# A hybrid attention layer on one core: where the inverses' transposes, the key norm's second half and the value copies stand in the queues

## The chip, the cores and the metric

The kernel runs on one core of a Trainium2 chip. A core has a matrix engine (TensorE, PE in the profile), VectorE (DVE), ScalarE (ACT), GpSimd (POOL) and SyncE (SP), each with a queue of its own that is worked off in order, and 16 DMA engines that move data. The metric is the device time of one execution in microseconds; less is better.

## The reference, cut to what matters

One layer of a diffusion backbone: 1,024 latent tokens and 256 context tokens of width 1,024. One input projection feeds two groups of heads; the rest (output projection, feed-forward) follows.

```python
px = modulate(rms_norm(x, norm1_w), sh1, sc1) @ w_in      # latent tokens; pc: the same for the context
qkv = short_conv(p[..., :3 * DN_WIDTH], conv_w)           # group A: gated DeltaNet, 4 heads, chunks
kb = k * beta[..., None]
m = jnp.where(strict, jnp.einsum("bhncd,bhnmd->bhncm", kb, k) * decay, 0.0)
a_mat = jnp.eye(CHUNK) + m
u = triangular_solve(a_mat, v * beta[..., None], ...)     # and w, from kb: a scan over the chunks follows
q = rms_norm(q, q_norm_w) * NA_HEAD_DIM ** -0.5           # group B: neighbourhood attention, 8 heads
k = rms_norm(k, k_norm_w)
k_r = lax.dynamic_slice_in_dim(kg, r0, win_rows, axis=1)[:, :, key_cols]
v_r = lax.dynamic_slice_in_dim(vg, r0, win_rows, axis=1)[:, :, key_cols]
```

`key_cols` are four overlapping blocks of 32 of the 64 grid columns; the values of each block are gathered over all 16 rows.

## The kernel before, in words

**The stage.** The change lies in the input projection, from about 100 to 550 us. The activations stand in SBUF as fp32r pairs, `hh` + `hl` (a high part and what is left), and each product is made of three: `whi*hh`, `whi*hl`, `wlo*hh`. The projection is a list of jobs. A `Block` gives 128 columns, transposed: `k`, `q`, `v`, `z` of group A, `nk` and `nq` (keys and queries) of group B. A `Wide` gives half of group B's values, which go to the DRAM tile `nv_d`. A block over latent tokens alone has two segments of 512 columns, so 8 x 3 x 2 = 48 products in two PSUM banks (`blk`, four in all); `nk` has a third segment of 256. The order of jobs around the change is `nk` 0, 1, 2, the second `Wide`, `nk` 3, `nq` 0, 1, 2, `q` 0.

**What goes with a job.** The weights of the next job are loaded by SP (`wraw`, one buffer), cast by ACT (`whi`, L219) and split by POOL (`wlo`, L221). A finished block is copied out of PSUM by ACT (`evac`, L491) into `cacc` (two buffers) and squared (L532). Its `norm` follows a job later: PE sums the squares (`m<-cr`, `pr<-cr`), ACT takes Ln and Exp (L549 to L553), DVE multiplies (L556), ACT casts to fp16 (L561, L568), DVE subtracts for the low half (L562, L569), and SP stores both to `nk_d` or `nq_d`.

**Beside the jobs.** Generators are advanced by `bg.step` after each of a job's eight steps. `block_inverses` inverts the triangular 32x32 blocks of group A for all chunks, heads and both directions at once: `N` holds them with the 80 blocks on partitions; 30 pairs of DVE operations (L947, L949) and a memset of the diagonal (L952) do the elimination; PE transposes `N` back, 32 transposes into `m` banks (L106 in the profile, a helper's line), DVE copies them to `WK` (L961); then for each direction DVE transposes 32x32 blocks (L967), SP stores to `x_d` (L969), DVE scales by beta (L970) and SP stores that (L972). `preps` then prepares each chunk of the scan: `fetch` loads `e`, `kk` and the inverses `xc`; POOL masks `e`; ACT copies `xc` into `fx` (L1011) and takes the exponentials of `e` (L1015); DVE multiplies `kk` by `e` (L1016); PE multiplies (`pr<-fx,kk` in the profile), and three rounds follow (`pr<-y,kk`, each copied by DVE, L1036). `windows` copies the four column blocks of the values from `nv_d` to `vw_d`, in 16 DMAs on SP, from the second `Wide` on.

**What sets the order.** The program is written in the order of these generators; a scheduler then sets each engine's queue from its own estimate of times and from priorities. `keep_in_program_order` pins an instruction where it is written, `high_priority` lets one go ahead of what is written before it, `issue_after` puts one behind another in its queue.

**PSUM and memory.** The banks `m` and `pr` are two each. Buffers are reused under waits: a tile's next user waits for the last one's reads and stores. DMAs share eight semaphores in turn, and one waits for the DMA before it on its semaphore.

## Time and profile before

| | |
|---|---|
| median of 3 runs | 1506.96 us (1506.89 to 1511.58) |
| the profiled execution's own time | 1507.78 us |
| its span, first to last instruction | 1506.0 us |
| PE busy | 1449.8 us, 96% of the span |
| DVE, ACT, POOL busy | 1004.4, 696.2, 193.4 us |
| mean granted clock of PE | 0.994 |
| DMA | 267.35 MB, mean 178 GB/s |

The profile is of one execution; its rows give start, duration, engine, line, operation, tiles written and read, shapes and count, and in brackets how long the engine was idle before and what ended that. A row can merge equal instructions that follow each other. Line numbers in the profile are those of the kernel before; in the changed one the same statements stand 5 to 11 lines further down at first, and some 20 at the end of the stage.

### The profile page before, as it was taken

Reading aid. Unit: us, or ns where it says so; the run is one execution under the profiler, and the core shown is the slowest. Engines: PE = TensorE matmul, PEld = TensorE weight load, DVE = VectorE, ACT = ScalarE, POOL = GpSimd, SP = SyncE. Lnnn points to the kernel's source line nnn. Section 1 sums busy time; section 2 is a strip of 40 time slices with the busy share of each in tenths; the row PEclk is TensorE's granted clock in tenths of the full one; section 3 lists DMA queues with packets and bytes.
Section 4 is the critical chain, followed back from the end, with each engine's and each line's share of the span. In section 5 each row is a group of like instructions: output and inputs, shape, how many; then the busy total and the mean of one; then the engine's idle time right before and its main releaser. Section 6 shows DMA issues by size and latency. Waiting matters only on the chain.

```text
span 1506.0 us, 23093 instructions
## 1 busy us (share of the span) xinstructions
PE 1449.8 (96%) x8365; PEld 1201.0 (80%) x8365; DVE 1004.4 (67%) x1892; ACT 696.2 (46%) x1321; POOL 193.4 (13%) x223
## 2 busy tenths in 40 slices
PE   5999998899999999999989999999999999999998
PEld 2789787678877778887877878888888888888887
DVE  4886579455598427679966499666655557698642
ACT  6443461584266526566742374333333334354440
POOL 0154500343124221211100000000000000000000
PEclk9999999999999999999999999999999999999999
DMA  9377133555377799986349106333333334898742
GB/s 368 117 234 239 57 92 121 191 168 190 118 243 238 220 284 265 262 228 193 110 134 332 72 30 203 113 105 105 102 102 105 106 105 161 287 349 286 240 145 84
DMA packets 198851, 267.35 MB, mean 178 GB/s; under 512 B 15232, under 2 KB 106960, under 8 KB 197712
## 3 DMA queue, kind: packets, MB, share of 16 engines
q1 hardware_dynamic: 198016, 265.49, 54.7%
q8 instruction: 66, 1.08, 0.3%
q14 instruction: 49, 0.40, 0.1%
q10 hardware_dynamic: 720, 0.37, 0.1%
HBM read 201.01 MB, written 68.98 MB: 179 GB/s over the span
## 4 chain that ended last, share of the span: by engine, by line
PE 51%; DVE 6%; ACT 3%; DMA 2%; issue 1%; SPq 0%; ACTq 0%; DVEq 0%
PE ps L102 45%; PE sc L102 5%; PE sc L106 2%; DMA wad<-wa 1%; ACT pt L377 1%; ACT ex L365 1%; DVE ex L363 1%; DVE acc L255 1%; DVE x L1618 1%; DVE x L1594 0%; DVE ex L367 0%; DVE ulo L1449 0%; DVE lT L1589 0%; DVE ws L1444 0%; ACT x L1598 0%
## 5 line engine op out<-in xcount | busy, mean ns | idle before, releaser
L102 PE MATMUL ps<-hT,uhi 128*128 128x512 f32 x496 | 146.8, 390 | 0.8 <-DVE e L1739 0.7
L102 PE MATMUL ps<-lT,uhi 128*128 128x512 f32 x496 | 146.4, 389 | 0.0
L102 PE MATMUL ps<-hT,ulo 128*128 128x512 f32 x496 | 146.3, 389 | 0.0
L102 PE MATMUL blk<-hh,whi 128*128 128x512 f32 (+1 forms) x456 | 138.0, 393 | 2.4 <-ACT hh L748 1.7
L102 PE MATMUL blk<-hh,wlo 128*128 128x512 f32 (+1 forms) x456 | 129.7, 377 | 0.0
L102 PE MATMUL ps<-hB,uhi 128*128 128x512 f32 x436 | 129.1, 390 | 0.0
L102 PE MATMUL blk<-hl,whi 128*128 128x512 f32 (+1 forms) x456 | 129.0, 376 | 0.0
L102 PE MATMUL ps<-lB,uhi 128*128 128x512 f32 x436 | 128.8, 389 | 0.0
L102 PE MATMUL ps<-hB,ulo 128*128 128x512 f32 x436 | 128.8, 389 | 0.0
L1448 ACT CAST uhi<-ws 128x512 fp32r<-128x512 f32 x91 | 54.7, 622 | 145.5 <-PE ps L102 78.2
L1448 ACT CAST uhi<-wq 128x512 fp32r<-128x512 f32 x101 | 60.4, 621 | 132.8 <-PE ps L102 69.4
L1449 DVE TENSOR_TENSOR ulo<-wq,uhi 128x512 fp32r<-128x512 f32 x101 | 67.1, 687 | 65.6 <-ACT uhi L1448 36.4
L102 PEld LDWEIGHTS ps<-hT,uhi 128*128 128x128 f32 x496 | 93.0, 188 | 20.7 <-ACT uhi L1448 1.1
L102 PEld LDWEIGHTS ps<-lT,uhi 128*128 128x128 f32 x496 | 93.0, 188 | 19.7 <-DVE lT L1602 0.5
L102 PEld LDWEIGHTS ps<-hT,ulo 128*128 128x128 f32 x496 | 93.1, 188 | 19.4
L102 PEld LDWEIGHTS ps<-hB,uhi 128*128 128x128 f32 x436 | 81.8, 188 | 17.5 <-issue 0.5
L102 PEld LDWEIGHTS ps<-lB,uhi 128*128 128x128 f32 x436 | 81.8, 188 | 17.3 <-DVE lB L1602 0.4
L102 PEld LDWEIGHTS ps<-hB,ulo 128*128 128x128 f32 x436 | 81.8, 188 | 17.0
L102 PEld LDWEIGHTS blk<-hh,wlo 128*128 128x128 f32 x456 | 80.1, 189 | 17.6 <-issue 1.7
L102 PEld LDWEIGHTS blk<-hl,whi 128*128 128x128 f32 x456 | 80.7, 189 | 15.5
L102 PEld LDWEIGHTS blk<-hh,whi 128*128 128x128 f32 x456 | 76.5, 189 | 19.8 <-ACT hh L748 3.7
L1449 DVE TENSOR_TENSOR ulo<-ws,uhi 128x512 fp32r<-128x512 f32 x91 | 60.6, 685 | 36.2 <-ACT uhi L1448 28.0
(341 smaller groups left out, 3026.0 us busy)
## 6 DMA issues: line engine op xcount, KB each, us to landing
wq<-w_fo SPq DMA_DIRECT2D x99, 256.0 KB
wq<-w_gu SPq DMA_DIRECT2D x88, 256.0 KB
wad<-wa SPq DMA_DIRECT2D x64, 256.0 KB
t_d<-g SPq DMA_DIRECT2D x22, 512.0 KB
fr<-t_d SPq DMA_DIRECT2D x44, 256.0 KB
bt<-rpb SPq DMA_DIRECT2D x48, 192.0 KB
f_d<-g SPq DMA_DIRECT2D x33, 256.0 KB
fr<-f_d SPq DMA_DIRECT2D x33, 256.0 KB
```

Of the source, the lines that this page charges most:

```text
L102: i = nc.tensor.matmul(*args, **kw)
L106: i = nc.tensor.transpose(*args, **kw)
L255: dve.scalar_tensor_tensor(acc2, x, sc, acc2, op0=OP.mult, op1=OP.add)
L363: dve.tensor_tensor_reduce(ex, sc, bt, 1.0, -3.0e38, OP.add, OP.max, m[:, 0:1])
L365: act.activation(ex, ex, AF.Exp, bias=m[:, 1:2], accum_out=m[:, 2:3])
L377: act.copy(pt, sc)
L1448: act.copy(hi, self.raw[key])
L1449: dve.tensor_tensor(lo, self.raw[key], hi.bitcast(F32), OP.subtract)
L1618: dve.tensor_tensor(B[at][:, k], B[x][:, k], B.get(y, B["B11"])[:, k], OP.subtract)
```

## The change

1. The inverses' transposes wait for eight steps of the background instead of one, are pinned where they are written, eight after each of four steps of the job `nq` 1; DVE's copies get a high priority.
2. The block transposes and scalings of both directions follow the copies with a high priority. The result `ut` now lies in the memory of `N`.
3. `norm` is split: its second half (`split`: L556 to L574 of before) of the last key block (`nk` 3, `tail`) is written after the inverse is done and the first fetch is issued, and issued behind the last scaling; the query blocks' second halves up to `turn` go behind it too.
4. The first two fetches of `preps` come ahead of its loop, with three steps of pause.
5. The value copies: `vw_d` is laid out as four blocks of 512 keys x 512 columns, each is copied by one DMA of 16 runs of 64 KB on ACT's queue, one at every second step of `nk` 3.

```diff
-    vw_d = dram.tile([128, 4, 4, 512], F32, name="vw_d", tag="vw_d")
+    vw_d = dram.tile([4, 512, 512], F32, name="vw_d", tag="vw_d")
...
+                return self.split
+            def split(self):
+                acc, t0, i, r = self.acc, self.t0, self.i, self.r
+                isk = self.kind == "nk"
                 u = acc
                 dve.scalar_tensor_tensor(u[:, t0:], u[:, t0:], qkw[:, isk:isk + 1], r[:, t0:],
...
-                for _ in range(1):
+                for _ in range(8):
                     yield
...
-                        pe.transpose(p[:, i * P:(i + 1) * P], N[:P, :, :, i0 + i].rearrange("p b r -> p (b r)"),
-                                     ident[:P, :P])
-                    dve.tensor_copy(U[:, :, i0:i0 + 4], p[:, :4 * P].rearrange("p (i u) -> p u i", i=4))
+                        tc.keep_in_program_order(nc.tensor.transpose(
+                            p[:, i * P:(i + 1) * P], N[:P, :, :, i0 + i].rearrange("p b r -> p (b r)"),
+                            ident[:P, :P]))
+                    with tc.high_priority(offset=400):
+                        dve.tensor_copy(U[:, :, i0:i0 + 4], p[:, :4 * P].rearrange("p (i u) -> p u i", i=4))
...
-                    ut = g4.tile([128, NU, 32], F32, name="ut", tag="ut")
+                with tc.high_priority(offset=400):
+                        ut = N.rearrange("p b r c -> p (b r c)")[:, d * 1280:(d + 1) * 1280].rearrange(
+                            "p (u i) -> p u i", i=32)
...
+                landing += [[fetch(*todo.pop(0)), False] for _ in range(2)]
+                for _ in range(3):
+                    yield
...
-                for ch in range(4):
-                    sp.dma_start(vw_d[:, cb, ch], vlat[4 * ch:4 * ch + 4, BLKS[cb]:BLKS[cb] + 32])
-                    yield
+                act.dma_start(vw_d[cb].rearrange("(r c) d -> r (c d)", c=32),
+                              vlat[:, BLKS[cb]:BLKS[cb] + 32].rearrange("r c d -> r (c d)"))
+                yield
...
-                    bg.step(1 if n < turn else 3)
+                    bg.step(1 if n < turn else 4 if k == 7 else 3)
                     bg2.step(1)
-                    copies.step(2)
+                    copies.step(k % 2)
+                if waiting:
+                    while not started:
+                        bg.step(1)
+                    with tc.issue_after(inverse[0].ins):
+                        waiting.pop()()
                 j.evac()
...
-                nrm.norm()
+                rest = nrm.norm()
+                if nrm is tail and not inverse:
+                    waiting.append(rest)
+                else:
+                    with tc.issue_after(inverse[0].ins) if inverse and n < turn else ExitStack():
+                        rest()
```

**PE, the transposes of N** (`hh_136` and `hl_137` are the activations' first tiles, `hh_423` and `hl_424` the last). Before, in the job `nq` 0, from its thirty-seventh product on:

```order
L102 MATMUL blk<-hh_419,whi 128x512 x2
L106 MATMUL m<-cst,N 128x80 x2
L102 MATMUL blk<-hl_420,whi 128x512 x2
L102 MATMUL blk<-hh_419,wlo 128x512
L106 MATMUL m<-cst,N 128x80 x6
L102 MATMUL blk<-hh_419,wlo 128x512
L102 MATMUL blk<-hh_421,whi 128x512
L106 MATMUL m<-cst,N 128x80 x4
```

Now, at the start of `nq` 1, behind the sums of the key norm (`m<-cr`, `pr<-cr`):

```order
L102 MATMUL m<-cr,cst 128x256
L102 MATMUL m<-cr,cst 128x512
L102 MATMUL pr<-cr,cst 128x512
L102 MATMUL blk<-hh_136,whi 128x512 x2
L102 MATMUL blk<-hl_137,whi 128x512 x2
L102 MATMUL blk<-hh_136,wlo 128x512 x2
L964 MATMUL m<-cst,N 128x80 x8
L102 MATMUL blk<-hh_138,whi 128x512 x2
L102 MATMUL blk<-hl_139,whi 128x512 x2
L102 MATMUL blk<-hh_138,wlo 128x512 x2
L964 MATMUL m<-cst,N 128x80 x8
```

The transposes went behind the rest of `nq` 0, the key norm's sums and six products, and come in four groups of eight.

**DVE, from the copies of the transposes to the first preparation's `kk*e`.** Before:

```order
L961 COPY WK<-m 128x80x4 x8
L967 STREAM_TRANSPOSE ut<-WK 128x1280
L970 TENSOR_TENSOR ut<-ut,NB 128x1280
L556 SCALAR_TENSOR_TENSOR cacc<-cacc,qkw,cr 128x1280
L967 STREAM_TRANSPOSE ut<-WK 128x1280
L562 TENSOR_TENSOR hl_2526<-cacc,hl_2526 128x1280
L970 TENSOR_TENSOR WK<-WK,NB 128x1280
L556 SCALAR_TENSOR_TENSOR cacc<-cacc,qkw,cr 128x1024
L1016 TENSOR_TENSOR kk<-kk,e 128x512 x2
```

Now:

```order
L968 COPY WK<-m 128x80x4 x8
L976 STREAM_TRANSPOSE N<-WK 128x1280 x2
L979 TENSOR_TENSOR N<-N,NB 128x1280
L979 TENSOR_TENSOR WK<-WK,NB 128x1280
L561 SCALAR_TENSOR_TENSOR cacc<-cacc,qkw,cr 128x1280
L561 SCALAR_TENSOR_TENSOR cacc<-cacc,qkw,cr 128x1024
L567 TENSOR_TENSOR hl_2556<-cacc,hl_2556 128x1280
L574 TENSOR_TENSOR hl_2574<-cacc,hl_2574 128x512 x2
L1026 TENSOR_TENSOR kk<-kk,e 128x512 x2
```

The transposes and scalings went ahead of the key norm; its subtraction and the query norm's two now stand ahead of `kk*e`.

**ACT, from the cast of `q` 0's weights to the exponentials of the first preparation.** Before:

```order
L219 CAST whi<-wraw 128x1024
L491 ACTIVATE cacc<-blk 128x512 x2
L549 ACT_TABLE_LOAD
L549 ACTIVATE cr<-m,bias 128x512 x2
L532 ACTIVATE cr<-cacc 128x1024
L551 ACT_TABLE_LOAD
L551 ACTIVATE cr<-cr,bias 128x1024
L1011 COPY fx_2478<-xc 32x4x32 x4
L1015 ACTIVATE e<-e,GN 128x128 x5
```

Now:

```order
L219 CAST whi<-wraw 128x1024
L549 ACT_TABLE_LOAD
L549 ACTIVATE cr<-m,bias 128x512 x2
L551 ACT_TABLE_LOAD
L551 ACTIVATE cr<-cr,bias 128x1024
L566 CAST hl_2556<-cacc 128x1280
L573 CAST hl_2574<-cacc 128x512 x2
L491 ACTIVATE cacc<-blk 128x512 x2
L1021 COPY fx_2523<-xc 32x4x32
L532 ACTIVATE cr<-cacc 128x1024
L1021 COPY fx_2523<-xc 32x4x32 x3
L1025 ACTIVATE e<-e,GN 128x128 x4
```

The key norm's cast and the query norm's two now stand ahead of the second query block's evacuation and of `fx`.

More of the change, by code (lines that the diff above doesn't have):

```diff
@@ L544, in norm @@
                     sp.dma_start(qT_d[:, i], acc[:, t0:])
-                    return
+                    return int
                 for s0, n in self.segs:
@@ L958, in block_inverses @@
                     for i in range(4):
-                        pe.transpose(p[:, i * P:(i + 1) * P], N[:P, :, :, i0 + i].rearrange("p b r -> p (b r)"),
-                                     ident[:P, :P])
-                    dve.tensor_copy(U[:, :, i0:i0 + 4], p[:, :4 * P].rearrange("p (i u) -> p u i", i=4))
+                        tc.keep_in_program_order(nc.tensor.transpose(
[3 more added lines that the diff above has]
+                        dve.tensor_copy(U[:, :, i0:i0 + 4], p[:, :4 * P].rearrange("p (i u) -> p u i", i=4))
                     if i0 % 8 == 4:
                         yield
-                for d in range(2):
-                    ud = U[:, d * NU:(d + 1) * NU]
-                    ut = g4.tile([128, NU, 32], F32, name="ut", tag="ut")
-                    dve.transpose(fl(ut), fl(ud))
-                    x, s = (ut, ud) if d else (ud, ut)
-                    sp.dma_start(x_d[:, d, 0], x)
-                    dve.tensor_tensor(s, s, NB[:, d].rearrange("p c (h o) -> p (c h) o", o=1).to_broadcast(
-                        [128, NU, 32]), OP.mult)
-                    sp.dma_start(x_d[:, d, 1], s)
-                    yield
-        done = set()
+                with tc.high_priority(offset=400):
+                    for d in range(2):
+                        ud = U[:, d * NU:(d + 1) * NU]
+                        ut = N.rearrange("p b r c -> p (b r c)")[:, d * 1280:(d + 1) * 1280].rearrange(
+                            "p (u i) -> p u i", i=32)
+                        dve.transpose(fl(ut), fl(ud))
+                        x, s = (ut, ud) if d else (ud, ut)
+                        sp.dma_start(x_d[:, d, 0], x)
+                        end = dve.tensor_tensor(s, s, NB[:, d].rearrange("p c (h o) -> p (c h) o", o=1).to_broadcast(
+                            [128, NU, 32]), OP.mult)
+                        sp.dma_start(x_d[:, d, 1], s)
+                inverse[:] = [end]
+                yield
+        done, inverse, waiting, started = set(), [], [], []
         def preps():
@@ L998, in fetch @@
                     sp.dma_start(kk, kk_d[:, c])
-                    sp.dma_start(xc, x_d[:, d, :, c * 4:c * 4 + 4])
+                    started.append(sp.dma_start(xc, x_d[:, d, :, c * 4:c * 4 + 4]))
                     at = None
@@ L1084, in hybrid @@
         later = len(jobs)
-        values = inv + 3
+        tail = jobs[inv + 4]
         queries = range(turn - 1, later)
@@ L1108, in hybrid @@
         first[1].evac()
-        first[0].norm()
+        first[0].norm()()
         first[1].silu()
@@ L1145, in hybrid @@
                     if t == 4 and nrm:
-                        nrm.norm()
+                        nrm.norm()()
                         for _ in fin:
@@ L1170, in hybrid @@
             done.add(n - 2)
-            if isinstance(j, Wide) and n == values:
+            if n == inv + 3:
                 copies.add(windows())
             if nrm:
-                nrm.norm()
+                rest = nrm.norm()
[4 more added lines that the diff above has]
+                        rest()
             if isinstance(j, Block) and j.later is None:
```

9 lines of the change are left out of this document (4 added, 5 removed).

## The prediction

> **What bounds the kernel.** TensorE (PE) is busy for nearly the whole span, so I first read the list of PE's waits to see where it is not. Between 225 and 550 us two waits are long, and both lie in the stage that the change rewrites. The first number is the total in us, then how often, then the longest.
>
> ```profile
> PE pr L102 <- DVE kk L1016: 6.9, 1, 6.9
> PE m L106 <- DVE N L952: 5.4, 1, 5.4
> ```
>
> The second came first in time: the inverses' transposes (L106, from N) stand in PE's queue before VectorE (DVE) has finished N. The other is the first scan preparation's matmul (`pr<-fx,kk`), waiting for DVE's `kk*e` (L1016). Next I read the stretches around both (from and to, length, busy us of PE, PEld, DVE, ACT, POOL, then the granted clock, DMA share, GB/s), since an idle PE also loses clock.
>
> ```profile
> 259.64:266.47 6.83, 4.06 (x18) 3.37 (x18) 4.27 (x11) 0.00 (x0) 0.00 (x0) 0.50 0.43 142
> 293.78:297.19 3.41, 0.00 (x0) 0.00 (x0) 1.11 (x1) 1.75 (x6) 2.06 (x6) 1.00 0.92 266
> 297.19:304.02 6.83, 4.93 (x22) 3.93 (x23) 1.90 (x4) 4.88 (x15) 3.74 (x11) 0.50 0.80 271
> 553.20:556.60 3.40, 1.37 (x11) 1.11 (x10) 1.90 (x11) 3.37 (x7) 0.00 (x0) 1.00 0.87 274
> 556.60:560.00 3.40, 3.40 (x17) 3.40 (x17) 1.28 (x3) 3.40 (x8) 1.04 (x1) 0.50 1.08 349
> 778.46:781.88 3.42, 1.72 (x7) 1.42 (x8) 1.36 (x3) 1.24 (x2) 0.00 (x0) 1.00 0.94 335
> 781.88:785.30 3.42, 3.42 (x16) 2.82 (x15) 0.37 (x1) 0.00 (x0) 0.00 (x0) 1.00 0.98 316
> 242.00:250.00 8.00, 8.00 (x42) 6.73 (x40) 7.76 (x8) 1.06 (x2) 0.00 (x0) 1.00 0.26 102
> ```
>
> Each wait is followed by 6.83 us at half clock, in which PE was busy 4.06 and 4.93 us; half of that is lost, 2.0 and 2.5 us. So the two waits cost 5.4 + 2.0 and 6.9 + 2.5, together 16.8 us. That is the ceiling of the gain. Once the preparations are through, the changed program's order on PE is the old one, so what is won here should reach the end.
>
> **Part 1: the transposes, 22 products later.** PE's rows (start, duration, idle before in brackets) give the new arrival.
>
> ```profile
> 249.28 0.40 PE L102 MATMUL blk<-hh,whi 128*128 128x512 f32 x1
> 262.41 0.53 PE L106 MATMUL m<-cst,N 80*128 80x80 f32 x2 [5.42 <-DVE N L952]
> 265.83 0.73 PE L106 MATMUL m<-cst,N 80*128 80x80 f32 x4
> 269.80 0.70 PE L102 MATMUL blk<-hh,whi 128*128 128x512 f32 x2
> 271.27 1.45 PE L102 MATMUL m<-cr,cst 128*128 128x256 f32 x4
> 273.02 1.04 PE L102 MATMUL blk<-hh,whi 128*128 128x512 f32 x2
> 273.90 0.63 PE L102 MATMUL blk<-hl,whi 128*128 128x512 f32 x2
> 284.37 1.88 PE L102 MATMUL m<-cr,cst 128*128 128x512 f32 x4
> 285.69 1.04 PE L102 MATMUL blk<-hh,whi 128*128 128x512 f32 x2
> 299.09 2.02 PE L102 MATMUL pr<-fx,kk 128*128 128x96 f32 x8 [6.90 <-DVE kk L1016]
> ```
>
> A job of 48 products takes 273.02 to 284.37 = 11.35 us; its first pair takes 0.88 and the other 23 take (284.37 - 273.90)/23 = 0.455. The first query block starts at 249.28, now with nothing between its products: 24 x 0.455 = 10.9, to 260.2. The key norm's products take 271.27 to 273.02 = 1.75, to 262.0, and three pairs of the next job 0.88 + 2 x 0.455 = 1.8. PE reaches the first transpose at 263.8. The 32 transposes themselves stay: 24 of them with 6 products took 265.83 to 269.80 = 3.97, so 0.11 us each, 3.5 in all, before and after.
>
> Is N ready at 263.8? DVE and GpSimd (POOL):
>
> ```profile
> 250.07 2.66 POOL L221 TENSOR_TENSOR wlo<-wraw,whi 128x1024 fp32r<-128x1024 f32 x1 [44.72 <-ACT whi L219]
> 250.49 3.02 DVE L947 TENSOR_TENSOR tt<-N 80x736 f32<-80x736 f32 x1
> 261.18 0.51 DVE L949 TENSOR_TENSOR N<-N,tt 80x336 f32<-80x336 f32 x1
> 262.93 0.28 DVE L949 TENSOR_TENSOR N<-N,tt 80x120 f32<-80x120 f32 x1
> 270.64 1.51 DVE L967 STREAM_TRANSPOSE ut<-WK 128x1280 f32<-128x1280 f32 x1
> 272.18 1.49 DVE L970 TENSOR_TENSOR ut<-ut,NB 128x1280 f32<-128x1280 f32 x1
> 282.04 1.55 DVE L556 SCALAR_TENSOR_TENSOR cacc<-cacc,qkw,cr 128x1280 f32<-128x1280 f32 x1 [8.36 <-ACT cr L553]
> 298.34 0.69 DVE L1016 TENSOR_TENSOR kk<-kk,e 128x512 f32<-128x512 f32 x1 [3.45 <-DMA nk_d<-hl]
> ```
>
> Before, N was ready at 263.21, which alone would just do. But the 3.02 us row beside POOL's 2.66 us one shows that such a DVE operation stands still while POOL splits weights. The next split came late before, because ScalarE (ACT) waited 20.93 us for its weights (second row below); that load stood in SyncE's (SP) queue behind the sixteen copies. With the copies gone, ACT casts as soon as PE lets go of the buffer, some 0.4 us ahead of the block's end, at 259.8 to 260.8, and POOL splits from 260.8 to 263.5, in front of N's last 263.21 - 261.18 = 2.0 us. So N is ready at about 265.5 and PE waits 1.7 us. Bounds: 0 (POOL misses the chain) to 3 (the load lands late and holds back ACT's Ln, which frees the bank the transposes write). I take 1.7.
>
> **Part 2: from the inverse to the first preparation.** ACT's rows:
>
> ```profile
> 248.94 1.05 ACT L219 CAST whi<-wraw 128x1024 fp32r<-128x1024 f32 x1 [13.14 <-PE blk L102]
> 273.49 1.05 ACT L219 CAST whi<-wraw 128x1024 fp32r<-128x1024 f32 x1 [20.93 <-DMA wraw<-w_nqk]
> 286.50 1.09 ACT L491 ACTIVATE cacc<-blk 128x512 f32<-128x512 f32 x2 [0.67 <-DVE hl L562]
> 288.90 1.27 ACT L549 ACTIVATE cr<-m,bias 128x512 f32<-128x512 f32 x2
> 290.06 1.06 ACT L532 ACTIVATE cr<-cacc 128x1024 f32<-128x1024 f32 x1
> 291.13 1.28 ACT L551 ACT_TABLE_LOAD   x1
> 292.43 1.15 ACT L551 ACTIVATE cr<-cr,bias 128x1024 f32<-128x1024 f32 x1
> 295.35 1.25 ACT L1011 COPY fx<-xc 32x128 f32<-32x128 f32 x4 [1.77 <-DMA xc<-x_d]
> 296.63 1.57 ACT L1015 ACTIVATE e<-e,GN 128x128 f32<-128x128 f32 x5
> ```
>
> The SP queue (issue times) and all sixteen of the old copies' issues (shortest, median, longest, in ns):
>
> ```profile
> 290.05 0.33 SPq L972 DMA_DIRECT2D x_d<-WK  x1
> 293.66 0.79 SPq L998 DMA_DIRECT2D kk<-kk_d  x2
> L1095 SPq DMA_DIRECT2D vw_d<-nv_d x16: 589/647/2513, 220.3 to 260.6; - x16
> ```
>
> The second query block with the transposes in it ends at E = 262.0 + 11.35 + 3.5 + 1.7 = 278.6. The last transposes are out some 5 us earlier, at 273, and the copies at 273.5. Two transposes (1.5) and two scalings (1.5), now back to back, end at 279.5; before, the second scaling ended at 290.0, behind the norm's 8.36 us wait. The last store has landed 293.66 - 290.05 = 3.6 us later, at 283.1. The first transpose's result now lies in N, so nothing waits for its store any more; but the new tiles e and kk lie where N and WK lay, and their loads wait for the stores. The last, kk, goes at 283.1 and was used 298.34 - 293.66 = 4.7 us after its issue at most: the data are there by 288. The six clears on POOL, which now wait for the same store, end sooner. That chain is 10 us earlier than before.
>
> ACT is then the late one. In its new order it runs, from E - 0.4: the cast 1.05, a table load 1.3, two Ln 1.2, a table load 1.3, Exp 1.15, to E + 5.6. DVE multiplies the query (1.55 for 1,280 columns, 1.25 for 1,024), then subtracts for the deferred key norm (1.5, by the scaling of the same size; it frees the buffer): E + 8.3. ACT evacuates the second query block 1.1, copies fx 1.25 with a square of 1.06 between, and takes four exponentials at 1.57/5 = 0.31: E + 12.95. DVE's `kk*e` 0.7: E + 13.7. PE needs 284.37 to 285.69 = 1.3 for the norm and 0.4 + 42 x 0.228 = 10.0 for the products ahead of it: E + 11.3. PE waits 2.4 us instead of 6.9. The bounds are 0 (ACT's steps overlap better) and 6.9 (the old wait). One more short wait, for the copy of the result behind eight more ACT steps, I put at 0.3, within 0 to 1.
>
> **Clock.** The two 1.7 and 2.4 us waits can still cost clock. The rows above show full clock behind a stretch with PE busy 1.72 of 3.42, half clock behind 1.37 of 3.40 and behind 0.00 of 3.41: idle for more than half of such a stretch loses the next one, at most 1.7 us. A 1.7 us wait does so in about half of its positions, a 2.4 us one in two thirds: 0.85 + 1.15 = 2.0 us. The Trainium skill (TensorE: Matmul & The Clock Gate, "Part 1: The HAM clock gate") has the half clock follow at least one idle window of about 3.4 us; by that neither wait would cost clock and the sum would be 2.0 us lower. The row at 553.20, half busy and yet followed by half clock, speaks against it.
>
> **Part 3: the copies.** Sixteen SP issues go, four ACT issues come. ACT holds them through the last store of the values, inside its idle 13.14 us ahead of 248.94: I cost them at nothing. That idle time begins at 235.8, when ACT has copied the last values; a store landed 3.6 us after its issue above, so the copies start near 239. If that cover goes, PE needs ACT's evacuation for the second half of the first query block, at 249.28 + 24 x 0.228 = 254.8; until then it is free. The old copies moved 102 GB/s on 0.26 of 16 engines, from four rows each; the new ones have sixteen rows. Their 4.2 MB take 41 us at the old rate, to about 281, or 10 us on all engines. Loads and stores of the stage share their semaphores, but even 281 is no later than the last x_d store lands.
>
> **Sum.** -16.8 + 1.7 + 2.4 + 0.3 + 2.0 = -10.4 us. The profiled execution took 1507.78, so 1497.4; it lies 0.8 over the median 1506.96, so I say 1497.
>
> **Rivals.**
> 1. Both waits go whole, clock included: ACT and POOL hit nothing. Then -16.8 + 0.3: 1490.5. For it: before, the data came last, not ACT. Chance 0.17.
> 2. The preparation's wait comes back in its old size, from ACT's longer queue or late x_d stores: 4.5 us more and 1.3 of clock: 1503. For it: ACT gains the key norm's cast and the query's two ahead of fx. Against: ACT was idle 1.77 us there. Chance 0.2.
> 3. Slower: ACT is held by the four issues. If one holds ACT until its megabyte has moved at the old rate, ACT is free at 239 + 41 = 280, PE idles from 254.8 to 280, 25 us, and the rest follows: 1507 - 16.8 + 25 + 2.0 = 1517. It starts to cost past 254.8 and has taken back the whole gain at 254.8 + 10.4 = 265. Against: the longest of SP's sixteen issues took 2.51 us, so four of them would end by 250. Chance 0.06. The Trainium skill (DMA: Bandwidth & Descriptors, "Why a DMA increments its semaphore by 16 and not by 1") lets the slowest dimension set how many engines a copy uses, so four rows get four, as the 0.26 shows, and sixteen would get sixteen; by that this rival falls.
> 4. The gain is given back where DMA is dense (0.87 at 553): no change. Chance 0.05.
>
> **Numbers.** The forecast keeps 0.52, with 1493 to 1501 as its own range. 0.3% is 4.5 us, about what a measurement tells from no change: under 1502.4 is faster. Faster: 0.52 + 0.17 + half of rival 2 = 0.79; same: the rest of it, rival 4 and a little of 3 = 0.16; slower 0.05. The range from 1490 to 1503.5 leaves out the ends of rivals 1 and 2, rival 3 and rival 4.
>
> **What will show it.** Right: the wait for N under 3 us with POOL's split beside the chain's end; the four stores of x_d within 280; the first preparation's matmul waiting on DVE for an ACT exponential, not for a load; no 6.83 us of half clock. Wrong: ACT standing in its DMA issues at 250, or a new wait over 4 us between 250 and 330.

## The result, and the profile after

Over 20 runs of each, the changed kernel took 1507.29 us (median) and the kernel before 1511.20; the ratio is 0.9976, with a 95% interval of 0.9965 to 0.9988. That is 3.6 us of 1511, where 10.4 were forecast. (Two of the three times known before the change were at the low end of these 20, so the ratio is compared with the forecast, and not the median with 1497.) The profiled execution took 1505.92 us, its span is 1504.1.

PE's list of waits, whole span (total in us, how often, longest), now has these two lines, and two shorter waits for N, where the 6.9 and the 5.4 us stood:

```profile
PE pr L102 <- DVE kk L1026: 3.5, 2, 2.5
PE pr L102 <- ACT kk L1038: 3.3, 1, 3.3
```

To weigh the stage I took two marks that both programs have: the first product of the query block `nq` 0 and the sums `m<-ones,cr`, which come after the fourth preparation in both. Between them PE does the same work. The first mark of before is the row at 249.28 in the prediction; the second, in PE's timeline of before (start, duration, what):

```profile
349.55 1.84 PE L102 MATMUL m<-ones,cr 128*128 128x1 f32 x16
```

And both of them in PE's timeline of after:

```profile
250.81 0.40 PE L102 MATMUL blk<-hh,whi 128*128 128x512 f32 x1
...
347.69 1.84 PE L102 MATMUL m<-ones,cr 128*128 128x1 f32 x16
```

The stretch between the marks in before (from and to, length, busy us of PE, PEld, DVE, ACT, POOL, then PE's clock, DMA share, GB/s):

```profile
249.28:349.55 100.27, 87.96 (x443) 67.81 (x442) 55.05 (x68) 63.70 (x117) 35.67 (x48) 0.93 0.56 177
```

And in after:

```profile
250.81:347.69 96.88, 88.98 (x444) 68.00 (x443) 59.16 (x69) 64.94 (x118) 37.54 (x49) 0.95 0.55 170
```

So the stage is 100.27 - 96.88 = 3.4 us shorter. PE's idle time fell from 12.3 to 7.9 us, by 4.4, and its busy time grew by 1.0. From the second mark to the end both spans need the same: 1506.0 - 349.55 = 1156.45 and 1504.1 - 347.69 = 1156.41. The changed profile reaches the first mark 1.5 us later, in a part of the program that is the same in both: it is 0.8 us behind at 31 us, and then has a stretch of half clock, from 32.70 to 36.11 us, that the profile before has not. The part that the change touches gains 3.4.

Where the 7.9 us are, row by row (PE's timeline of after; the brackets are the idle time before):

```profile
266.22 0.42 PE L964 MATMUL m<-cst,N 80*128 80x80 f32 x2 [0.78 <-DVE N L957]
266.99 0.90 PE L964 MATMUL m<-cst,N 80*128 80x80 f32 x6 [0.35 <-DVE N L954]
...
295.31 1.85 PE L102 MATMUL pr<-fx,kk 128*128 128x96 f32 x8 [2.48 <-DVE kk L1026]
...
312.07 1.10 PE L102 MATMUL pr<-fx,kk 128*128 128x96 f32 x8 [1.04 <-DVE kk L1026]
...
327.25 1.03 PE L102 MATMUL pr<-fx,kk 128*128 128x96 f32 x8
...
332.94 0.57 PE L102 MATMUL pr<-y,kk 128*32 128x32 f32 x8 [3.25 <-ACT kk L1038]
```

The transposes wait 1.1 us for N and the first preparation 2.5 us, both about as forecast. The new one is the last: the fourth preparation's `pr<-y,kk` stands six products behind its `pr<-fx,kk` and waits 3.25 us for the copy of that result. Why the copy is late is read from ACT's timeline of after:

```profile
327.70 1.28 ACT L1025 ACTIVATE e<-e,GN 128x128 f32<-128x128 f32 x4
330.50 0.99 ACT L1025 ACTIVATE e<-e,GN 128x128 f32<-128x128 f32 x3 [1.52 <-POOL e L1054]
331.39 1.12 ACT L573 CAST hl<-cacc 128x512 f16<-128x512 f32 x2
332.42 0.47 ACT L1038 COPY kk<-pr 128x384 f32<-128x384 f32 x1
```

And from POOL's:

```profile
321.96 1.68 POOL L1022 COPY y<-xc 32x128 f32<-32x128 f32 x3 [5.62 <-DMA xc<-x_d]
323.71 2.38 POOL L221 TENSOR_TENSOR wlo<-wraw,whi 128x1024 fp32r<-128x1024 f32 x1
...
328.97 1.50 POOL L1054 TENSOR_SCALAR_AFFINE_SELECT e<-e 128x512 f32<-128x512 f32 x1
```

The result is there at 327.25 + 1.03 = 328.3. In ACT's queue seven exponentials and two casts of other work stand ahead of its copy. Before, nothing stood there: ACT was idle for 2.04 us ahead of the same copy and took it as soon as PE had the result (ACT's timeline of before), and PE did not wait.

```profile
327.93 0.48 ACT L1028 COPY kk<-pr 128x384 f32<-128x384 f32 x1 [2.04 <-PE pr L102]
```

In after, three of those exponentials wait for a mask that POOL has ready at 330.5; it comes behind a split and, ahead of that, a wait of 5.62 us for `xc`. That load is late because of SP's queue (issues, start and time that each took):

```profile
297.50 0.60 SPq L1007 DMA_DIRECT2D e<-g_d  x1
310.54 2.55 SPq L579 DMA_DIRECT2D nq_d<-hl  x4
...
316.36 0.59 SPq L218 DMA_DIRECT2D wraw<-w_conv  x1
...
317.71 0.42 SPq L1009 DMA_DIRECT2D xc<-x_d  x1
```

From 298.1 to 310.5 SP stands at a query block's store, whose data are not made yet, then at a load of weights until POOL's buffer is free, and the loads of the next preparations are behind both.

Behind three of the waits the clock fell. Six stretches of after, and one at 309.18 that kept its clock (columns as above):

```profile
264.80:268.21 3.41, 2.28 (x13) 1.64 (x12) 2.72 (x7) 3.39 (x5) 0.78 (x1) 1.00 0.26 78
268.21:271.62 3.41, 3.41 (x15) 2.80 (x14) 1.07 (x3) 1.53 (x2) 0.00 (x0) 0.50 0.28 80
292.10:295.51 3.41, 0.93 (x6) 0.47 (x4) 0.69 (x1) 3.31 (x12) 2.13 (x7) 1.00 0.90 250
295.51:298.92 3.41, 3.41 (x13) 2.57 (x13) 0.69 (x1) 1.83 (x6) 0.64 (x1) 0.50 0.89 267
329.65:333.06 3.41, 0.15 (x4) 0.12 (x4) 1.35 (x3) 2.53 (x7) 1.94 (x6) 1.00 0.84 274
333.06:336.48 3.42, 3.42 (x15) 2.78 (x15) 2.98 (x5) 3.37 (x9) 0.76 (x1) 0.50 0.80 188
309.18:312.59 3.41, 2.37 (x14) 1.74 (x12) 2.04 (x4) 3.34 (x11) 0.00 (x0) 1.00 0.28 61
```

The first and the last of these, with the tile `blk` alone (the products of 512 columns):

```profile
264.80:268.21 3.41, 1.17 (x5) 0.72 (x4) 0.00 (x0) 0.00 (x0) 1.00 0.26 78
309.18:312.59 3.41, 1.85 (x9) 1.19 (x7) 0.00 (x0) 0.00 (x0) 1.00 0.28 61
```

Three stretches at half clock, each with PE busy throughout: 3 x 3.41/2 = 5.1 us lost, against 4.5 before. So the change took 4.4 us of waiting away and lost slightly more to the clock than before.

### The profile page after: what moved, and what is told of

The parts are those of the page before. It is cut to its first block, busy times and chain, and to the rows that moved or that the text cites. A ratio compares the mean times of both kernels' runs of the same rounds, so it can differ in the third digit from the quotient of the medians.

```text
span 1504.1 us, 23085 instructions
## 1 busy us (share of the span) xinstructions
PE 1453.2 (97%) x8365; PEld 1204.4 (80%) x8365; DVE 1007.5 (67%) x1892; ACT 698.8 (46%) x1323; POOL 197.0 (13%) x223
## 4 chain that ended last, share of the span: by engine, by line
PE 52%; DVE 6%; issue 3%; ACT 3%; DMA 2%; SPq 0%; ACTq 0%; DVEq 0%
PE ps L102 45%; PE sc L102 5%; PE sc L106 2%; ACT pt L377 1%; DMA wad<-wa 1%; ACT ex L365 1%; DVE ex L363 1%; DVE x L1641 1%; DVE acc L255 1%; DVE x L1617 0%; DVE ulo L1472 0%; DVE lT L1612 0%; DMA wq<-w_gu 0%; ACT x L1621 0%; DVE lB L1625 0%
## 5 line engine op out<-in xcount | busy, mean ns | idle before, releaser
L102 PEld LDWEIGHTS ps<-hT,uhi 128*128 128x128 f32 x496 | 92.9, 188 | 21.3 <-ACT uhi L1471 1.8
```

Source lines behind the costliest of these rows:

```text
L102: i = nc.tensor.matmul(*args, **kw)
```

## The experiments

Theory A: the gain is made where the prediction put it, and a single new wait, set by the place of one copy in ACT's queue, gives part of it back. Theory B: ACT, POOL and SP set the pace of the first four preparations as a whole, so that what PE wins ahead of them it waits for in them. All ratios are to the kernel before, with their 95% interval. "Stage" is the stretch between the two marks in a kernel's own profile (before 100.27, after 96.88), "idle" PE's idle time in it, "rest" its span less the second mark (both 1156.4), "last y" the start of the last multiplication of the first four preparations, counted from the first mark, which stands between 248.9 and 254.4 us in these profiles. These four columns are of one execution each; one stretch of half clock more or less is 1.7 us in them.

| | ratio | stage | idle | rest | last y |
|---|---|---|---|---|---|
| before | 1 | 100.3 | 12.3 | 1156.4 | 86.1 |
| changed | 0.9976 (0.9965 to 0.9988) | 96.9 | 7.9 | 1156.4 | 89.1 |
| e1, changed, second profile | | 96.9 | 8.1 | 1156.0 | 89.1 |
| e2, fourth copy on DVE | 0.9951 (0.9933 to 0.9969) | 94.2 | 6.7 | 1153.4 | 87.0 |
| e3, copies as before | 1.0062 (1.0039 to 1.0085) | 109.7 | 20.6 | 1153.8 | 101.8 |
| e4, copies alone | 1.0126 (1.0103 to 1.0149) | 117.4 | 28.8 | 1160.6 | 103.2 |
| e5, e2 and transposes later | 0.9962 (0.9949 to 0.9975) | 95.5 | 8.6 | 1152.6 | 87.5 |
| e6, e2 and first `fx` on DVE | 0.9950 (0.9937 to 0.9964) | 93.5 | 6.2 | 1157.9 | 86.4 |
| e7, key norm not split | 0.9969 (0.9957 to 0.9980) | 94.9 | 6.9 | 1155.5 | 87.3 |
| e8, no pause | 0.9960 (0.9947 to 0.9973) | 96.0 | 6.9 | 1156.0 | 86.4 |
| e9, rule for all | 1.0032 (1.0020 to 1.0044) | 92.1 | 6.0 | 1171.1 | 83.9 |
| e10, e9 and transposes later | 1.0020 (1.0003 to 1.0036) | 92.8 | 6.9 | 1169.4 | 85.0 |
| e11, e10 without split | 1.0016 (1.0003 to 1.0028) | 91.3 | 5.4 | 1169.5 | 83.6 |
| e12, slack | 0.9954 (0.9938 to 0.9970) | 93.0 | 5.3 | 1159.9 | 88.6 |
| e13, rule for two | 0.9980 (0.9965 to 0.9996) | 98.6 | 8.3 | 1158.2 | 90.4 |
| e14, e13 and transposes later | 0.9947 (0.9931 to 0.9962) | 92.5 | 6.6 | 1160.0 | 84.5 |
| e15, e13 without split | 0.9988 (0.9974 to 1.0003) | 95.2 | 7.3 | 1162.1 | 87.0 |
| e16, all three | 0.9992 (0.9977 to 1.0008) | 97.1 | 8.0 | 1161.9 | 89.5 |
| e17, `fx` on DVE | 0.9962 (0.9942 to 0.9982) | 93.0 | 8.3 | 1155.7 | 84.7 |
| e18, e17 and transposes later | 0.9938 (0.9914 to 0.9962) | 94.3 | 7.9 | 1157.7 | 85.8 |

**e1, the changed kernel again.** No edit.

> The changed kernel once more, unedited, for a second profile. Theory A (the gain is there at 325 us and is given back by one new wait, PE's pr<-y,kk for ScalarE's copy of the fourth preparation's result, 3.25 us at 329.7 and 1.7 us of half clock behind it): the same wait stands at the same place in PE's order, 2.5 to 4 us, and PE's lead over the kernel before falls there by 4 to 6 us. Theory C (the loss is chance of that one execution, by where the clock's windows fall): another wait is the longest, or this one is under 1.5 us.

The same wait stands at the same place in PE's order, 3.50 us long, and the stage was 96.9 us again. The new wait belongs to the program and is not chance.

**e2, one copy moved.**

```diff
-                    act.copy(f[:, :, s], ...)
+                    if n == 3:
+                        with tc.high_priority(offset=400):
+                            dve.tensor_copy(f[:, :, s], ...)
+                    else:
+                        act.copy(f[:, :, s], ...)
```

> The changed kernel with one instruction moved: the copy of the fourth preparation's result out of PSUM is done by VectorE, behind its convolution step that ends at 330.0, instead of by ScalarE behind seven exponentials and two casts. Theory A: the wait of 3.25 us falls to 0.9 at most and the half clock behind it goes: 4 us faster than the changed kernel (1503 against 1507), ratio to the kernel before about 0.995. Theory B (ScalarE, GpSimd and SyncE set the pace of the preparations as a whole, so that what PE gains it must wait for): a wait of 3 to 4 us comes back within the next two preparations and the time is that of the changed kernel, ratio 0.9976.

It took 0.9951, 0.0025 below the changed kernel, or 3.8 us; the two intervals just touch, and e6, which has the same edit, lies clear of the changed kernel. The copy now ends at 330.3, and PE's wait is 1.16 us with no half clock behind it (timeline of e2):

```profile
329.71 0.56 DVE L1040 COPY kk<-pr 128x384 f32<-128x384 f32 x1
...
330.32 0.44 PE L102 MATMUL pr<-y,kk 128*32 128x32 f32 x8 [1.16 <-DVE kk L1040]
```

This is nearly as theory A had it, which allowed 0.9 us. ACT's exponentials waited for their mask as long as in the changed kernel (1.52 us); only no multiplication waited behind them. The stage shrank by 96.9 - 94.2 = 2.7 us, about the 3.25 - 1.16 = 2.1 of waiting and the 1.7 of clock, less a further wait of 0.9 that came in their place.

**e3, the copies as before.** Part 5 undone in the changed kernel.

```diff
-                act.dma_start(vw_d[cb].rearrange("(r c) d -> r (c d)", c=32), ...)
-                yield
+                for ch in range(4):
+                    sp.dma_start(vw_d[:, cb, ch], vlat[4 * ch:4 * ch + 4, BLKS[cb]:BLKS[cb] + 32])
+                    yield
```

> The changed kernel with part 5 undone: the value copies are sixteen on SyncE's queue again, in the old layout. Theory A (the copies on ScalarE gain nothing by themselves, and cost N's last steps the collision with GpSimd's split): VectorE's last steps on N run undisturbed, N is ready 2 us earlier, PE's waits for N (1.1 us) go, all else as in the changed kernel: 0 to 2 us faster than it, ratio to before 0.996 to 0.998. Rival (the copies hold back the weights and the stores on SyncE's queue, and that is what the change gains by): 4 us slower than the changed kernel, ratio about 1.000.

Theory A was wrong: 1.0062, 13 us slower than the changed kernel, the way of the rival and three times its 4 us. In its list of waits:

```profile
PE m L964 <- ACT cr L549: 13.6, 1, 13.6
```

And in its timeline, SP's issue and ACT's cast:

```profile
261.30 2.57 SPq L218 DMA_DIRECT2D wraw<-w_nqk  x1
...
273.74 1.04 ACT L219 CAST whi<-wraw 128x1024 fp32r<-128x1024 f32 x1 [21.30 <-DMA wraw<-w_nqk]
```

The weights' load goes out behind the sixteen copies, ACT stands 21.3 us at their cast, and the Ln that reads the key norm's sums (L549) is behind the cast. The transposes use the same two `m` banks as those sums, and they now come after them, so PE waits 13.6 us. Before, the transposes came ahead of the sums, and the late cast held nobody on PE. Whether the copies' new queue gains anything by itself this does not show, but without it the later transposes lose.

**e4, the copies alone.** Part 5 in the kernel before, all else as it was.

> The kernel before with part 5 alone: four copies of 16 runs of 64 KB on ScalarE's queue. Theory A: the 5.4 us wait for N stays, since the transposes still stand in the first query block; the preparation's first matmul, whose place in PE's order comes earlier, still waits 4 to 7 us: within 3 us of the kernel before, ratio 0.998 to 1.002. Rival (the copies are the gain): ratio 0.9976 or less.

It took 1.0126: 19 us slower, against both expectations. ACT's timeline of e4 shows its DMA issues (ACTq) and what stands behind them:

```profile
241.56 1.19 ACTq L1094 DMA_DIRECT2D vw_d<-nv_d  x2
...
286.17 1.12 ACTq L1094 DMA_DIRECT2D vw_d<-nv_d  x2
287.33 1.36 ACT L491 ACTIVATE cacc<-blk 128x256 f32<-128x256 f32 x3 [49.96 <-DMA xc<-x_d]
```

And PE's:

```profile
287.77 0.80 PE L102 MATMUL blk<-hh,whi 128*128 128x512 f32 x1 [19.79 <-ACT cacc L491]
```

Two of the four copies are issued at once and the other two 43.4 us later. In between ACT does nothing: the evacuation of the key block is behind the third issue in its queue, and PE waits 19.79 us for that evacuation. This is the prediction's third rival, ACT held by its issues, though not by the transfer, since the copies land 5.8 to 10.7 us after their issue. The profile names a load of the inverses (`xc`, on SP's queue) as what ended ACT's wait. That a DMA waits for the one before it on its semaphore would fit; which semaphore it was, no view here shows. In the changed kernel all four issues are over at 244.0.

So parts 1 to 4 without part 5 (e3) lose, and part 5 without the others (e4) loses. Which of the four keeps ACT's issues free was not tried, and e4 does not give the price of the copies by themselves.

**e5, the transposes 28 products later, on top of e2.**

```diff
-                for _ in range(8):
+                for _ in range(9):
                     yield
```

> The kernel of the second experiment (fourth copy on VectorE, ratio 0.9951) with the transposes of N one step of the job later, 28 products instead of 22 behind their old place. Theory A (PE's two short waits for N, 1.1 us together, cost a stretch of half clock as well, 1.7 us, because the transposes beside them hardly count as work): both go, no half clock near 267: 2.8 us faster than the second experiment, less up to 1.4 if the preparations come that much later: ratio 0.993 to 0.9945. Theory B (the preparations' pace on ScalarE decides, what PE wins ahead of it is waited for behind): the wait for kk (2.5 us at 293) grows by what was won: ratio 0.995.

The waits for N and the half clock near 267 are gone, as theory A had it. But the ratio is 0.9962, no better than e2, as theory B had it. The orders behind the transposes changed too, and the wait is again at the fourth preparation's copy, now on DVE (timeline of e5):

```profile
327.16 2.34 POOL L221 TENSOR_TENSOR wlo<-wraw,whi 128x1024 fp32r<-128x1024 f32 x1 [8.02 <-ACT whi L219]
327.63 2.42 DVE L574 TENSOR_TENSOR hl<-cacc,hl 128x512 f16<-128x512 f32 x1 [0.33 <-ACT hl L573]
329.98 0.55 DVE L1040 COPY kk<-pr 128x384 f32<-128x384 f32 x1
330.44 0.68 DVE L574 TENSOR_TENSOR hl<-cacc,hl 128x512 f16<-128x512 f32 x1
330.58 0.64 PE L102 MATMUL pr<-y,kk 128*32 128x32 f32 x8 [4.85 <-DVE kk L1040]
```

One half of the subtraction takes 2.42 us beside POOL's split and 0.68 behind it, and the copy stands behind it. The Trainium skill (SBUF — State Buffer, "SBUF: two separate sides") calls the port pair of the two engines an exclusive lock, held for a whole instruction; the rows agree: the slow half ends 0.55 us behind the split (330.05 against 329.50), not quite the 0.68 that the other half takes undisturbed.

**e6, the first preparation's `fx` copies on DVE, on top of e2.**

> The kernel of the second experiment with the four copies of the first preparation's fx on VectorE instead of ScalarE (1.2 us off ScalarE's queue). Theory B (ScalarE's queue sets when the first preparation can be multiplied): its exponentials end 1.2 us earlier, VectorE's product too, and PE starts pr<-fx at 294.0 instead of 295.2: 0.5 to 1.2 us faster than the second experiment, ratio about 0.9945. Rival (that product waits for a load or for the query norm on VectorE): PE starts it at the same time or later, ratio 0.995 to 0.996.

The ratio is that of e2 (0.9950). In its profile the first `pr<-fx` stands 43.3 us behind the first mark instead of 44.5, 1.2 us earlier, as theory B had it, and the stage is 0.6 us shorter. PE came to it 0.9 us earlier too, since four products fewer stand ahead of it, so the wait only fell from 2.47 to 2.18 us. ACT's queue does set when that product can start, but 0.6 us are below what the ratio tells.

**e7, the key norm's second half where it was (part 3 undone).**

```diff
-                rest = nrm.norm()
-                if nrm is tail and not inverse:
-                    waiting.append(rest)
-                else: ...
+                nrm.norm()()
```

> The changed kernel with part 3 undone: the key norm's second half is issued where it was, ahead of the inverse's last copies. Theory A (the gain comes from the order of transposes and copies; the norm's split is worth the 8.36 us wait that stood between the two scalings only if VectorE would wait there): with the sums of the norm now 1.5 us after the second query block's start, ScalarE's exponential is ready by 270 and VectorE would hardly wait: within 2 us of the changed kernel, ratio 0.9965 to 0.999. Rival (the split carries the gain): 4 us slower or more, ratio 1.000 and up.

It took 0.9969, the same as the changed kernel within the intervals. DVE's old 8.36 us wait for the exponential does not come back (DVE's timeline of e7):

```profile
267.88 1.55 DVE L561 SCALAR_TENSOR_TENSOR cacc<-cacc,qkw,cr 128x1280 f32<-128x1280 f32 x1 [1.38 <-ACT cr L553]
```

With the transposes later the norm's sums come first, and 1.38 us between two of DVE's copies cost PE 0.20. In this order part 3 won nothing that part 1 had not won; in that of e16 it did (below).

**e8, without the pause (part 4 undone).** The three steps of pause were taken out; the loop would issue the two fetches first anyway.

> The changed kernel with part 4 undone: no two fetches ahead of the loop and no pause of three steps. Theory A (the loss at 330 us comes from where the scheduler puts the fourth preparation's copy in ScalarE's queue, which part 4 sets): the copy stands elsewhere, the 3.3 us wait is gone or stands with another preparation: 0 to 4 us faster than the changed kernel, ratio 0.995 to 0.998. Rival (the pause is what lets the first preparation's data arrive): PE waits 5 us and more for the first pr<-fx, ratio 0.999 to 1.001.

It took 0.9960, between changed and e2 and told apart from neither. The time is in theory A's range, but its mechanism did not come: PE waits 3.08 us for ACT's copy of the same fourth preparation.

**e9 to e11, a rule on ACT's queue.** Later exponentials are issued behind the copy written before them; e10 has the transposes later as well, e11 also part 3 undone.

```diff
-                    for h in range(4):
-                        act.activation(e[:, h], e[:, h], AF.Exp, bias=GN[:, d, c, h:h + 1])
+                    with tc.issue_after(last[0].ins) if last else ExitStack():
+                        for h in range(4):
+                            act.activation(e[:, h], e[:, h], AF.Exp, bias=GN[:, d, c, h:h + 1])
...
-                    act.copy(f[:, :, s], ...)
+                    last[:] = [act.copy(f[:, :, s], ...)]
```

> The changed kernel with one rule added on ScalarE's queue: a later preparation's exponentials are issued behind the copy of the result that was written before them. Theory A (the gain is given back where ScalarE's queue puts the fourth preparation's copy behind exponentials whose mask is late): the wait of 3.25 us for that copy and its half clock go, as with the copy on VectorE: ratio 0.994 to 0.996. Theory B (the pace of ScalarE's work as a whole): the wait comes back for another instruction of the preparations, ratio 0.997 to 0.998.

> The kernel with that rule and the transposes 28 instead of 22 products behind their old place. Theory A: the waits for N (1.1 us, half clock 1.7) go as well and are not given back: 2 us faster than with the rule alone, ratio 0.992 to 0.9945. Theory B: ratio 0.995 to 0.997, the same as the other versions.

> The kernel with the rule and the later transposes, and the key norm's second half where it was before the change (part 3 undone): its cast and its subtraction no longer stand ahead of the first preparation's exponentials. Theory A (ScalarE ends the first preparation's chain): the wait of 2.5 us for the first product of kk and e shrinks by up to 1.2: ratio 0.991 to 0.994. Theory B: 0.995 to 0.997.

All three are slower than the kernel before, against both theories, though their stages are among the shortest: 92.1, 92.8 and 91.3 us, 7.5 to 9 below before. The loss is in the rest, 13 to 15 us longer. The rule also binds the sixteen preparations after the fourth; PE's waits from the second mark to 556 us in e9 are, by its list:

```profile
PE ps L102 <- ACT zt L483: 4.6, 1, 4.6
PE pr L102 <- DVE kk L1027: 4.4, 4, 2.2
```

The first was 1.0 in the changed kernel, the second not there. Of the 14.7 us that e9's rest is longer, 6.5 are idle time of PE (29.3 us against 22.8) and 8.2 are busy time, at a mean granted clock of 0.99 against 1.00.

**e12, slack instead of a rule.** Transposes later, and one more step of the background between copy and next multiplication in the first six preparations.

> The changed kernel with the transposes 28 products later and, in the first six preparations, one more step of the background between a result's copy and the next multiplication; no rule on ScalarE's queue. In PE's order the fourth preparation's y then stands 12 products behind its fx instead of 6. Theory A (six products are 1.4 us and ScalarE needs 5): 12 products are 2.7 us, the wait shrinks by 1.4 at least: ratio 0.993 to 0.9955. Theory B (the later steps of the preparations then hold up what follows): 0.996 to 0.998.

It took 0.9954, in theory A's range and not told apart from e2. In its profile PE does not wait at the fourth preparation at all; its idle time in the stage, 5.3 us, is the least of all versions.

**e13 to e16, the rule for the fifth and sixth preparation only.** Edit as in e9, with `if last and n in (4, 5)`; e14 has the transposes later, e15 part 3 undone, e16 both.

> The changed kernel with the rule of the ninth experiment for the fifth and sixth preparations alone, so that ScalarE's queue stays as it was for all later ones. In the ninth experiment PE was 8.0 us ahead of the kernel before at 345 us (lead since 250 us) and lost 10 us between 430 and 550, where the rule put the later preparations' exponentials behind copies. Theory A (the wait at 330 is the loss, and the rule's reach made the ninth slow): lead of 6 to 8 us at 345, kept to the end, ratio 0.9945 to 0.9955. Theory B (the rule as such delays the exponentials, and the preparations as a whole are at their pace): the lead falls back behind 345, ratio 0.997 and up.

> The same with the transposes 28 products later. Theory A: the waits for N (1.1 us) and their half clock (1.7) go and are kept: ratio 0.9925 to 0.9945. Theory B: 0.996 and up.

> The kernel of the thirteenth experiment with part 3 undone (the key norm's second half where it was). The seventh experiment found part 3 worth nothing by itself. Theory A: within 1.5 us of the thirteenth, ratio 0.994 to 0.996. Rival (the split holds the gain together once the wait at 330 is gone): 3 us slower, 0.997 and up.

> The rule for two preparations, the transposes 28 products later and part 3 undone, all in one. In the eleventh experiment, which had the rule for all preparations, the lead since 250 us was 8.9 us at 345, the largest of all. Theory A: kept to the end, ratio 0.992 to 0.9945, the fastest of the versions. Theory B: 0.996 and up.

With the rule cut to two preparations the rest is 1158 to 1162, and e13's ratio is 0.0052 below e9's, so the rule's reach was most of e9's loss. But e13's stage is 98.6, longer than the changed kernel's: a wait of 2.2 us at the fourth preparation's copy, and one of 1.5 us just ahead of that preparation, for an earlier one's last round, took the place of the one. e14 gained; e13, e15 and e16 lie between the changed kernel and the one before. Theory A's numbers are nearly met in e14 alone (0.9947, expected up to 0.9945); the other three lie in theory B's ranges.

e16 against e14 also shows what part 3 is for: with the transposes later, undoing part 3 costs 0.0045, or 6.8 us, and the intervals lie apart. DVE's wait for the norm's exponential is back there, 2.84 us long, between the elimination and the copies of the transposes, and PE waits for those copies (PE's timeline of e16):

```profile
272.56 1.12 PE L964 MATMUL m<-cst,N 80*128 80x80 f32 x8 [2.00 <-DVE WK L968]
```

The rest of the 6.8 us is not traced; other waits changed too.

**e17 and e18, ACT's work.** The `fx` copies of the first six preparations on DVE, in the changed kernel and with later transposes.

```diff
-                        act.copy(fx[q, :, q], xc[q, 1])
+                        (dve.tensor_copy if n < 6 else act.copy)(fx[q, :, q], xc[q, 1])
```

> The changed kernel with the fx copies of the first six preparations on VectorE: some 24 copies of 0.29 us, 7 us, leave ScalarE's queue between 281 and 340 us. In all kernels so far the last multiplication of the first four preparations starts between 334 and 341 us, wherever the first one starts (291.5 to 299.1). Theory B (ScalarE's work sets that pace): it starts at 334 or earlier, the wait for the fourth copy shrinks to 1 us, ratio 0.994 to 0.9955. Theory A (only the place of single instructions in the queues decides, and VectorE's queue is as full): it starts at 336 to 341 again, ratio 0.996 to 0.999.

> The same with the transposes of N 28 products later. Theory B: ratio 0.992 to 0.994, the fastest version. Theory A: the waits for N go, the wait at the fourth preparation stays at 3 us or more, ratio 0.9945 to 0.997.

These two leave the question open. The last multiplication starts at 336.8 and 336.3, in theory A's range; but e17's first mark stands 1.3 us later than that of the changed kernel, and counted from the marks the last multiplication comes 4.4 us earlier (84.7 against 89.1). The fourth copy's wait fell to 1.30 us, near theory B's 1. Yet PE's idle time in the stage is 8.3 us, against 7.9: the third preparation now waits 2.07 us instead of 1.04, and an earlier one's last round 1.65. What e17 gains in its stage is clock, a mean of 1.00 against 0.95, and at least at the wait for N that hangs on where the stretches fall (last section). So 7 us less work on ACT moved the waits and did not shorten them in sum, while the interval of e17's ratio covers both theories' ranges.

e18 is the fastest version that was run, 1501.98 us, 0.9938, in theory B's range; its interval lies clear of the changed kernel's, and overlaps theory A's range and those of e2, e14 and others. In it PE still waits 2.75 us for the fourth preparation's copy, and 4 us later once more, for 2.23 us.

**What stays open.** In all versions with the copies on ACT's queue and the transposes moved, the last multiplication of the first four preparations starts 83.6 to 90.4 us behind the first mark, as in the kernel before (86.1), although the first of them starts 40.9 to 44.5 us behind it instead of 49.8. PE's idle time in the stage is 5.3 to 8.6 us in all of them, against 7.9 in the changed kernel: an edit that takes one wait away mostly finds another. So theory A holds for the single wait (e2), and theory B may hold for what is left. A chain over four queues (SP's fetches behind a query block's store, POOL's masks behind its splits, ACT's and DVE's copies behind casts) is what the rows show; which link would have to go, no run told. Moving the fetches ahead of that store was not tried.

## Why the prediction was wrong

Its sum was -16.8 + 1.7 + 2.4 + 0.3 + 2.0 = -10.4. With what the terms measured: -16.8 + 1.1 + 2.5 + (1.04 + 3.25) + 5.1 = -3.8; the two marks give -3.4, and 20 runs -3.6. Two terms were mis-sized: the one for later waits by 4.0 us and the clock by 3.1.

**The wait for N: right.** Forecast 1.7 us, measured 1.1, by the cause given: POOL splits beside DVE's last steps on N (timeline of after).

```profile
262.87 2.71 POOL L221 TENSOR_TENSOR wlo<-wraw,whi 128x1024 fp32r<-128x1024 f32 x1 [7.54 <-ACT whi L219]
263.37 2.47 DVE L952 TENSOR_TENSOR tt<-N 80x232 f32<-80x232 f32 x1
```

**The first preparation: right.** The wait was forecast at 2.4 us and measured at 2.48, on DVE for an exponential of ACT. The profile names a store as what released DVE, but DVE starts 0.09 us behind the fourth exponential's end, as it does at the next preparation, where the exponential is named (timelines of after).

```profile
293.20 1.28 ACT L1025 ACTIVATE e<-e,GN 128x128 f32<-128x128 f32 x4
294.57 0.69 DVE L1026 TENSOR_TENSOR kk<-kk,e 128x512 f32<-128x512 f32 x1 [2.83 <-DMA nq_d<-hl]
```

The block's end E was 281.4 instead of 278.6, because the first mark came 1.5 us later and half clock stood behind the transposes; counted from there, PE arrived at E + 11.4 (forecast 11.3) and the product started at E + 13.9 (forecast 13.7).

**The step that failed: "one more short wait, for the copy of the result behind eight more ACT steps, I put at 0.3, within 0 to 1".** The thing was named, and its size was not worked out: later waits came to 4.3 us instead, 1.04 at the third preparation and 3.25 at the fourth. I priced it at the first preparation and took the later ones to be as before; but the order that sets their places had changed as well. In PE's order of before 24 products stand ahead of the fourth `pr<-fx`, now 6, and ACT's queue has seven exponentials ahead of the copy, where before ACT was idle. e2 shows that the largest wait hangs on the place of one copy, e5, e8 and e13 that a wait comes back at the same preparation. "What is won here should reach the end" was right from the second mark on, and wrong for the preparations that lie between.

**The clock: mis-sized, 2.0 forecast, 5.1 measured.** Chances of a half and two thirds were put on two waits; both lost their stretch, and the new wait a third. The trace's own rule (idle for over half of a stretch) failed at 264.80: PE was idle for 1.1 of 3.41 us there, and half clock followed. That one also hung on chance: with the same wait, e7, e9, e15 and e17 kept their clock (last section). The rule of the Trainium skill (TensorE: Matmul & The Clock Gate, "Part 1: The HAM clock gate"), at least one idle window ahead of half clock, would have given a loss of nothing at all three; the three stretches had PE busy for 2.28, 0.93 and 0.15 us, so the trace disagrees with it, further than with mine.

**The copies at nothing: right as far as it goes.** In this kernel ACT issued them in the idle time named, long before it was needed, so the third rival (ACT held, 1517 us) did not come. ACT's timeline of after:

```profile
241.56 2.47 ACTq L1107 DMA_DIRECT2D vw_d<-nv_d  x4
```

In e4 it did come, by a wait of the issue and not by the time of the transfer that the rival reckoned with. What I did not see is what the copies are for: e3 shows 13 us of loss without them, through the bank that the Ln frees. The prediction has that mechanism as the upper bound of the wait for N, at 3 us.

**Part 3 priced as a gain of the chain: not needed in this order** (e7), but needed in that of e16.

**Rivals and signs.** The second rival (0.2) came nearest, 4 us below before: a wait comes back from ACT's longer queue, with half clock behind it. Its place was wrong, the first preparation instead of the third and fourth. The fourth rival (the gain given back where DMA is dense) did not come, since the rest is as long as before. Of the signs of being right the stores of `x_d` failed, the last being issued at 282.29 instead of within 280; the other three came. Neither sign of being wrong came: the new wait of 3.25 us stayed under the 4 us set for it, so that sign was set too high for a sum with a term of 0.3.

## What to carry to other kernels

When a change moves a stage forward, price every instruction of the stage's following rounds and not the first alone: in in-order queues a scheduler may place a short copy behind work that waits for something else, and the matmul behind it then pays the whole wait and the half clock. Ask of each part of a change what it protects: a part that gains nothing may be what keeps another from losing (here a DMA queue, through a shared PSUM bank). Compare places in two profiles from a mark that both have, not from the start. And where one wait comes back in many forms, look for the chain over all queues ahead of moving single instructions.

## What was not expected of the hardware

Half clock followed a stretch with PE busy for 2.28 of 3.41 us, and full clock one with 2.37 (from 309.18). In the first, products of 512 columns took 1.17 us and the rest were transposes of 80 rows and columns; in the second the products took 1.85, beside the preparations' own.

The same wait of 1.1 us for N stands in ten profiles, each time in a stretch with PE busy for 2.28 to 2.33 us. In six of them (after, e1, e2, e6, e8, e13) the products of 512 columns took 1.17 to 1.19 us of it, and half clock followed. In the other four (e7, e9, e15, e17) they took 1.34 to 1.50, with fewer transposes, and the clock stayed. e17's stretch, whole and then with `blk` alone:

```profile
265.40:268.81 3.41, 2.28 (x13) 1.57 (x11) 2.73 (x6) 3.38 (x6) 1.48 (x1) 1.00 0.04 11
265.40:268.81 3.41, 1.34 (x6) 0.75 (x4) 0.00 (x0) 0.00 (x0) 1.00 0.04 11
```

So some 0.2 us in where a stretch begins decided over 1.7 us. This fits if such transposes hardly count as activity, but no run tried that by itself; e5, which took the idle 1.1 us away and kept the transposes, had no half clock there.

A program's time also varies with where the stretches fall. In e9's profile half clock followed a stretch at 113.56 with PE busy for 1.36 of 3.41 us, in a part that is the same in all these programs; in before the corresponding stretch, at 112.87, had PE busy for 2.19 us and kept its clock. This may be part of why the 20 runs of one program spread over 1502.55 to 1512.41 us.
